# Where the sums for four conditioning vectors stand in the first mixer, and how many weight tiles they have

## The chip, the cores and the metric

One core of a Trainium2 chip. The metric is the device time of one execution in microseconds, the median of repeated runs. The core has TensorE (PE, with its weight loads PEld), VectorE (DVE), ScalarE (ACT), GpSimd (POOL) and SyncE (SP); POOL and SP issue most of the DMA transfers.

## What is computed

A two-layer trunk over 512 latent tokens and 256 context tokens, model width 1024, in float32. Layer 0 mixes tokens with a Fourier mixer beside a short gated convolution; layer 1 with windowed attention. Each layer ends in a mixture of 32 experts. Six vectors per layer and per stream shift, scale and gate the sub-layers, computed from the conditioning vectors:

```python
mod_l = (jax.nn.silu(c) @ w_mod[layer] + b_mod[layer])[:, None, :]
mod_c = jax.nn.silu(c_ctx) @ w_mod[layer] + b_mod[layer]
sh1_l, sc1_l, g1_l, sh2_l, sc2_l, g2_l = jnp.split(mod_l, 6, axis=-1)
```

The change concerns four of those of layer 1, `g1_l` to `g2_l` (numbers 2 to 5), each a product of one 1024 vector with a 1024 x 1024 block of `w_mod`. In layer 1 only the latent stream needs them.

## The kernel before

The kernel is one stream of Python calls on the five engines; a framework sets the order of each engine's instructions (the code's order is their priority, and a later one whose data is ready may go first) and puts in the waits. Tiles come from pools with a number of buffers per name; one more tile of a name waits until an older one is released. `tc.issue_after(ins)` orders the instructions issued in its block behind `ins`, those on the engine of `ins` alone.

**Modulation by TensorE** (`ModFeed`, L999). Twelve 2 MB tiles w of `w_mod` are loaded through POOL's queue (L1015) into two slots in turn, after four through SP's. Each `feed.step` multiplies one tile (L1037, 16 matmuls) and issues the load of the tile after next. These steps are called the modulation steps below.

**Modulation by VectorE** (`SumFeed`, L1047). The four vectors of layer 1 go as 32 steps, eight for each vector. A step takes one 512 KB tile mw of weights (loaded through POOL's queue, L1068; pool `sp`, two buffers), multiplies it by a number per partition and adds it to acc (L1077 for the first of eight, L1075 for the others), and issues the next load. After the eighth, `finish` (L1082) loads the bias row into another mw tile, sums acc over partitions with four matmuls (L1088, the column sum), adds the bias (two ops at L1090) and writes the vector to memory (L1091). acc is a single buffer.

**First mixer.** Eight chunks follow each other, each with projections of the normed tokens (`proj`, L1247: weights split into a high half by ScalarE at L1253 and a low half by VectorE at L1255, three buffers each; 48 matmuls at L1259 and L1260). The four Fourier chunks (g = 0 to 3, L1309) have one projection each and the Fourier matmuls and sums of the chunk before (`four_b`, L1269: L1276 on TensorE, U copied by ScalarE at L1277, Z by VectorE at L1281 to L1295, L1299 and L1302 on TensorE). The four convolution chunks (j = 0 to 3, L1330) have three projections each, and VectorE's ops for the gated convolution (L1350 to L1360). Two or three `feed.step` and, before the change, one to three `sums.step` stand in each chunk. Pool `fp` holds the Fourier tables, U and Z; it is closed in the first convolution chunk, and `cp` takes its memory.

**Behind the mixer**, `mixer_out` (L1368) splits the output weights (L1402, L1403), multiplies (L1436), reads gates and router vectors that the modulation wrote (gr L1395, md L1383; br L1374 is a bias row of the router), and the experts of layer 0 follow. Their weights are loaded by SP.

Of the kernel before, what the change touches and what calls it, by code (L numbers as in the profile page):

```python
# [10 lines left out]
F32 = mybir.dt.float32  # L11
# [9 lines left out]
D = 1024  # L21
# [64 lines left out]
def body(tc, I, out, upto=None, dbg=None):  # L86
# [3 lines left out]
    def pool(name, bufs=1, side="left", space=None):  # L90
        kw = dict(name=name, bufs=bufs, reuse_waits="tile")
        if space is None:
            kw["side"] = side
        else:
            kw["space"] = space
        g = tc.tile_pool(**kw)
        p = g.__enter__()
        p_close[id(p)] = g
        return p
# [146 lines left out]
    class Route:  # L246
# [7 lines left out]
        def __init__(self, NT, tb, t, psum, acc, spill, quads=0):  # L254
            self.NT, self.tb, self.t, self.psum, self.spill, self.quads = NT, tb, t, psum, spill, quads
            self.pairs = 16 - 2 * quads
            self.blocks = self.pairs + quads
            self.early = FIXED if quads else 16
            self.lower = []
            self.cuts = CUTS[NT]  # L260
            self.lg = t([128, NT, 36])
            self.gm = t([128, NT])
            self.og = t([128, NT, 4])
            self.mx = t([128, 2, NT, 4])
            self.M = t([128, 2, NT, 32])
            self.Mb = t([128, NT, 32], BF)
            self.Mc = t([128, 32], BF)
            self.rk = t([128, 2, NT])
            self.R = t([128, 2, NT, 32])
            self.oh = t([128, 2, NT, 64], BF)  # L270
            self.Mv = t([128, 2, 2, NT, 32], BF)
            n = max(b - a for a, b in zip((0,) + self.cuts, self.cuts + (NT,)))
            self.kg, self.gk, self.km = t([128, n, 4]), t([128, n]), t([128, n, 4])
            self.d, self.k, self.s2 = [t([128, n, 4, 8]) for _ in range(3)]
            self.acc = acc([128, 2, self.early])
# [723 lines left out]
    class ModFeed:  # L999
# [20 lines left out]
        def step(self, again=-1):  # L1020

            if self.cp >= len(self.todo):
                return
            l, g, q = self.todo[self.cp]
            w, i = self.wt.pop(self.cp)
            self.cp += 1
            if q == 0:
                bsrc = I["b_mod"][l, g * 2048:(g + 1) * 2048].rearrange("(q n) -> q n", q=4)
                for s in range(2):
                    G.dma_start(bm[s:128:32, :], bsrc)  # L1030
            first, last = (q == 0, q == 3) if self.whole else (True, True)
            if first:
                self.ps = self.psum_tile()
            for kk in range(2):
                k = 2 * q + kk
                for cb in range(4):
                    T.matmul(self.ps[cb * 32:cb * 32 + 32, :], sil[:, k, :], w[:, kk, cb * 512:cb * 512 + 512],  # L1037
                             start=first and kk == 0, stop=last and kk == 1)
            if again is not None:
                self.load(i if again < 0 else again)  # L1040
            if last:
                self.sum = V.tensor_add(bm, self.ps, bm)
            if q == 3:
                for s in range(2):
                    G.dma_start(mod_d[l, s, g * 2048:(g + 1) * 2048].rearrange("(q n) -> q n", q=4), bm[s:128:32, :])

    class SumFeed:  # L1047
# [1 line left out]


        def __init__(self, layer, vectors, room):
            self.layer, self.vectors, self.room = layer, vectors, room
            self.acc = room.tile([128, D], F32, name="acc")
            self.todo = [(v, k) for v in vectors for k in range(8)]
            self.w = []
            self.ld = 0
            for _ in range(2):
                self.load()

        def tile(self):  # L1060
            return self.room.tile([128, D], F32, name="mw", bufs=2)

        def load(self):
            if self.ld < len(self.todo):
# [5 lines left out]
        def step(self):  # L1070
            v, k = self.todo.pop(0)
            self.ld -= 1
            w = self.w.pop(0)
            if k:
                V.scalar_tensor_tensor(self.acc, w, sil[:, k, 0:1], self.acc, op0=ALU.mult, op1=ALU.add)  # L1075
            else:
                V.tensor_scalar(self.acc, w, sil[:, k, 0:1], None, op0=ALU.mult)  # L1077
            if k == 7:
                self.finish(v)
            self.load()  # L1080

        def finish(self, v):  # L1082

            ps, b = psB([128, 512]), self.tile()
            rows = b[0:64:32, 0:512]
            G.dma_start(rows, I["b_mod"][self.layer, v * D:(v + 1) * D].rearrange("(q n) -> q n", q=2))
            for r in (0, 32):
                T.matmul(ps[r:r + 32, :], onef.to_broadcast([128, 32]), self.acc[:, r * 16:r * 16 + 512], start=True, stop=True)  # L1088
            for r in (0, 32):
                V.tensor_add(b[r:r + 1, 0:512], ps[r:r + 1, :], b[r:r + 1, 0:512])  # L1090
            G.dma_start(mod_d[self.layer, 0, v * D:(v + 1) * D].rearrange("(q n) -> q n", q=2), rows)  # L1091
# [88 lines left out]
    mm = {}  # L1180
# [29 lines left out]
    sp = pool("sp", side="right")  # L1210
# [20 lines left out]
    def proj_pre():  # L1231
        ps = [psA([128, L + LC]) for _ in range(2)]
        for s in range(2):
            for g in range(2):
                if s == 0 and g == 1:
                    with tc.issue_after(mm["hi", 0, 4].ins):
                        split_pre(1)
                out = ps[g][:, s * L:L + s * LC]
                for i, (w, h) in enumerate(((0, hhi), (1, hhi), (0, hlo))):
                    for k in range(8):  # L1240
                        mm["last"] = T.matmul(out, wpre[:, g, w, k, :], h[s][:, k, :], start=k == 0 and i == 0, stop=k == 7 and i == 2)
            if s == 0:
                with tc.issue_after(mm["last"].ins):
                    feed.step()
        return ps
# [17 lines left out]
    def four_a(g):  # L1263
        ps = pre[g] if g < 2 else proj(lambda k0: wraw[:, k0:k0 + 4, g * 128:(g + 1) * 128])
        aT = tp.tile([128, L + LC + 4], F32, name="t3", bufs=2)
        S.copy(aT[:, 0:L + LC], ps)
        return aT
# [37 lines left out]
    prev = None  # L1305
    load_conv(0)
    pre = proj_pre()
    sums = SumFeed(1, (2, 3, 4, 5), sp)
    for g in range(4):  # L1309
        aT = four_a(g)  # L1310
        if g:
            with tc.issue_after(mm["last"].ins):
                feed.step()
        sums.step()
        if prev is not None:
            four_b(g - 1, prev)
        feed.step()
        sums.step()
        sums.step()
        prev = aT  # L1320
    wo = I["w_out_even"][0].rearrange("(j p) d -> p j d", p=128)

# [7 lines left out]
    for j in range(4):  # L1330
        wr4 = wconv[j]
        pc = proj(lambda k0: wr4[:, k0:k0 + 4, 1, :])
        if prev is not None:
            four_b(3, prev)
            prev = None
            close(fp)
            cp = pool("cp")
            u = cp.tile([128, L + LC + 4], F32, name="ut")
            for c in (0, L + 1, L + 2, L + LC + 3):
                V.memset(u[:, c:c + 1], 0.0)  # L1340
        csb = tp.tile([128, L + LC + 4], F32, name="t3", bufs=2)
        S.copy(csb[:, 0:L + LC], pc)
        feed.step()
        sums.step()
        load_conv(j + 1)
        if j == 3:
            wout = load_wout(0, 1)
        phv = proj(lambda k0: wr4[:, k0:k0 + 4, 2, :])
        for o, p0, n in segs:
            V.tensor_mul(u[:, o:o + n], csb[:, p0:p0 + n], phv[:, p0:p0 + n])  # L1350
        z = cp.tile([128, L + LC + 4], F32, name="z", bufs=2)
        S.activation(z[:, 1:1 + N2], u[:, 1:1 + N2], AF.Copy, scale=cw[:, 1, j:j + 1])
        V.scalar_tensor_tensor(z[:, 1:1 + N2], u[:, 0:N2], cw[:, 0, j:j + 1], z[:, 1:1 + N2], op0=ALU.mult, op1=ALU.add)
        V.scalar_tensor_tensor(z[:, 1:1 + N2], u[:, 2:2 + N2], cw[:, 2, j:j + 1], z[:, 1:1 + N2], op0=ALU.mult, op1=ALU.add)
        feed.step()
        sums.step()
        sums.step()
        pb = proj(lambda k0: wr4[:, k0:k0 + 4, 0, :])
        for o, p0, n in segs:
            V.tensor_mul(z[:, o:o + n], z[:, o:o + n], pb[:, p0:p0 + n])  # L1360
        put_y(4 + j, [z[:, o:o + 256] for o in (1, 257, L + 3)])
        feed.step()
        sums.step()
        sums.step()
    close(cp, tp, sp, hp)


# [646 lines left out]
```

## Time and profile before

| | |
|---|---|
| median of 3 runs | 1658.29 us (1654.82 to 1658.82) |
| profiled execution, its own time | 1657.86 us |
| its span | 1655.9 us |
| TensorE busy | 1525.1 us (92%) |
| VectorE busy | 759.7 us (46%) |
| ScalarE / POOL busy | 440.3 us / 141.7 us |
| DMA, mean over the span | 304 GB/s |

The span is that of one execution taken by the hardware profiler. An engine is busy while one of its instructions runs; instructions that issue DMAs are not counted as busy in this table. The time from a DMA's issue to its landing is given apart. Matmuls are pipelined and their ends are modelled. In a timeline the bracket at the end of a row gives the idle time before it and what ended it.

### The profile page before, as it was taken

How to read it: one execution, taken by the hardware profiler on the slowest of the kernel's cores; microseconds unless marked ns; L12 is line 12 of the kernel's file. 1: busy time of each engine (PE TensorE's matmuls, PEld its weight loads, DVE VectorE, ACT ScalarE, POOL GpSimd, SP SyncE). 2: the span in 40 equal slices, each digit the busy share in tenths (PEclk: the TensorE clock that was granted, in tenths of full speed). 3: DMA queues.
4: the chain of work that ended last, by engine and by line, in shares of the span. 5: the costliest groups of instructions: out<-in, count | busy, mean ns of one | idle time of the engine just before them, and what ended most of it. 6: DMA issues, size and time to landing. Idle time of an engine off the chain costs nothing.

```text
span 1655.9 us, 21500 instructions
## 1 busy us (share of the span) xinstructions
PE 1525.1 (92%) x8011; PEld 866.5 (52%) x8011; DVE 759.7 (46%) x1671; ACT 440.3 (27%) x879; POOL 141.7 (9%) x160
## 2 busy tenths in 40 slices
PE   4989997969999999999988989999799999997787
PEld 2757876843444434444447776668444544531332
DVE  4546553784342534333366975555622322320223
ACT  5322221311111111111046577644221222210110
POOL 2522100300000000000033210000000000000000
PEclk9999997979999999999979999999899999998999
DMA  9897672579999999999930121042699999999996
GB/s 387 306 389 246 229 245 82 189 278 424 425 424 424 381 394 424 425 424 424 407 121 1 51 52 52 1 128 76 237 426 427 426 426 427 426 416 427 426 427 260
DMA packets 108832, 503.50 MB, mean 304 GB/s; under 512 B 18784, under 2 KB 33632, under 8 KB 56752
## 3 DMA queue, kind: packets, MB, share of 16 engines
q1 hardware_dynamic: 93600, 447.31, 67.1%
q0 software_dynamic: 11952, 51.55, 8.2%
q10 hardware_dynamic: 3168, 3.17, 0.6%
q8 instruction: 66, 1.08, 0.3%
q14 instruction: 46, 0.38, 0.1%
HBM read 499.30 MB, written 5.32 MB: 305 GB/s over the span
## 4 chain that ended last, share of the span: by engine, by line
PE 34%; DMA 10%; DVE 3%; ACT 2%; issue 1%; SPq 0%; DVEq 0%; ACTq 0%
PE p L862 8%; PE yp L933 5%; DMA w<-in_w_dram 5%; DMA hhi<-in_w_dram 4%; PE A L1715 3%; PE cp L811 3%; PE A L1436 3%; PE tp L767 2%; PE A L1833 2%; PE O L1895 2%; PE B L1880 2%; ACT P L1839 1%; PE tp L774 1%; DVE x L812 1%; DMA w<-in_w_qkv_dram 0%
## 5 line engine op out<-in xcount | busy, mean ns | idle before, releaser
L862 PE MATMUL p<-w,xt 128*64 128x512 f32 (+1 forms) x1024 | 338.5, 611 | 14.3 <-DMA w<-in_w_dram 14.1
L862 PE MATMUL p<-r,xt 128*64 128x512 f32 (+1 forms) x784 | 284.2, 620 | 8.3 <-DMA r<-in_w_dram 7.9
L812 DVE TENSOR_TENSOR x<-x,cp 128x512 f32<-128x512 f32 x224 | 148.1, 685 | 96.5 <-PE cp L811 96.4
L875 DVE TENSOR_TENSOR sg<-sg,p 128x512 f32<-128x512 f32 x29 | 20.0, 688 | 365.9 <-PE p L862 354.9
L811 PE MATMUL cp<-y,ot 128*128 128x512 f32 x616 | 174.5, 419 | 8.3 <-DVE x L812 4.5
L862 PEld LDWEIGHTS p<-w,xt 128*64 128x64 f32 (+1 forms) x1024 | 99.6, 135 | 127.3 <-issue 98.6
L933 PE MATMUL yp<-w,ht 128*64 128x512 f32 (+1 forms) x512 | 158.7, 595 | 2.2 <-DMA w<-in_w_dram 2.2
L862 PEld LDWEIGHTS p<-r,xt 128*64 128x64 f32 (+1 forms) x784 | 84.5, 137 | 144.5 <-issue 124.8
L811 PEld LDWEIGHTS cp<-y,ot 128*128 128x128 f32 x616 | 107.2, 191 | 52.0 <-DVE x L812 26.3
L933 PE MATMUL yp<-r,ht 128*64 128x512 f32 (+1 forms) x368 | 128.7, 595 | 1.3 <-ACT ht L894 0.7
L799 ACT CAST y<-yp 128x512 fp32r<-128x512 f32 x58 | 34.0, 586 | 277.0 <-DVE yp L795 185.5
L1436 PE MATMUL A<-r,r 128*128 128x512 f32 x288 | 71.2, 404 | 2.2 <-ACT r L1402 1.4
L933 PEld LDWEIGHTS yp<-r,ht 128*64 128x64 f32 (+1 forms) x368 | 38.1, 134 | 66.7 <-issue 64.0
L862 PE MATMUL p<-hhi,xt 128*64 128x512 f32 (+1 forms) x128 | 66.0, 672 | 7.1 <-DMA hhi<-in_w_dram 7.1
L933 PEld LDWEIGHTS yp<-w,ht 128*64 128x64 f32 (+1 forms) x512 | 46.4, 131 | 45.6 <-issue 40.1
L1436 PEld LDWEIGHTS A<-r,r 128*128 128x128 f32 x288 | 55.1, 195 | 14.8 <-ACT r L1402 2.3
L1837 DVE CUSTOM_DVE_ANT_0 A<-A,band,nsink 128x640 f32<-128x640 f32 (+1 forms) x56 | 45.4, 831 | 35.4 <-PE A L1833 35.2
L865 ACT ACTIVATE sg<-p 128x512 f32<-128x512 f32 x29 | 17.3, 597 | 157.0 <-PE p L862 157.0
L801 DVE TENSOR_TENSOR y<-yp,y 128x512 fp32r<-128x512 f32 x58 | 40.1, 691 | 40.0 <-ACT y L799 40.0
L797 DVE SCALAR_TENSOR_TENSOR yp<-yp,gs,grow 128x512 f32<-128x512 f32 x26 | 19.7, 759 | 72.4 <-PE yp L933 72.4
L739 POOL DMA_INDIRECT r<-h_d,gi x17 | 17.0, 997 | 411.8 <-PE tp L774 342.4
L862 PE MATMUL p<-hlo,xt 128*64 128x512 f32 (+1 forms) x112 | 51.8, 611 | 0.0
(434 smaller groups left out, 2605.5 us busy)
## 6 DMA issues: line engine op xcount, KB each, us to landing
w<-in_w_dram SPq DMA_DIRECT2D x191, 1024.0 KB, 19.5
r<-in_w_dram SPq DMA_DIRECT2D x143, 1024.0 KB, 19.5
w<-in_w_mod_dram POOLq DMA_DIRECT2D x12, 2048.0 KB, 10.1
hhi<-in_w_dram SPq DMA_DIRECT2D x23, 1024.0 KB, 19.5
hlo<-in_w_dram SPq DMA_DIRECT2D x23, 1024.0 KB, 19.5
mw<-in_w_mod_dram POOLq DMA_DIRECT2D x32, 512.0 KB, 5.2
w<-in_w_in_even_dram SPq DMA_DIRECT2D x13, 512.0 KB, 11.2
w<-in_w_mod_dram SPq DMA_DIRECT2D x3, 2048.0 KB, 12.8
```

The source lines that it names most:

```text
L767: T.matmul(p, oh[:, m, :], near["h2"][m][i][:, hf * 512:hf * 512 + 512], start=n == 0, stop=n == 7)
L799: hi = S.copy(Yr[j, hf][0], ys)
L801: V.tensor_sub(Yr[j, hf][1], ys, Yr[j, hf][0].bitcast(F32))
L811: T.matmul(p, OT[j][:, m * 128:(m + 1) * 128], Yr[j, hf][i], start=n == 0 and i == 0, stop=n == len(js) - 1 and i == 1)
L812: return V.tensor_add(xs, xs, p)
L862: T.matmul(ps[rs], X[b][:, q, rs], W[j, wn, ab][:, q, :], start=q == 0, stop=q == 7)
L933: T.matmul(py_[hf][rs, :], HT[b][:, q % 4, rs], W[j, "w2", ab][:, q % 4, hf * 512:hf * 512 + 512], start=q % 4 == 0, stop=q % 4 == 3)
L1436: T.matmul(ps, lhs(m, a, j), whl[b][:, j, :], start=j == 0 and i == 0, stop=j == 7 and i == 2)
L1715: T.matmul(ps, h[st][:, k, ms], whl[k][b], start=k == 0 and i == 0, stop=k == 7 and i == 2)
L1833: T.matmul(ps[:, o0:o0 + w], qS[G_][:, c, b * 128:(b + 1) * 128], kS[part][:, 2 * G_ + c // 4, k0:k0 + w], start=part == 0, stop=part == 1)
L1837: V.tensor_tensor_reduce(out=ps[:, 0:w], in0=ps[:, 0:w], in1=bnd, op0=ALU.add, op1=ALU.min, scale=1.0, scalar=nsink[:, hd:hd + 1], accum_o ...
L1880: T.transpose(p[:, i, :], Ps[gl * 4 + i][:, t * 128:(t + 1) * 128], ident)
```

## The change

The object that holds the sums is made in the first Fourier chunk instead of ahead of the four, in an `issue_after` block that names the last matmul so far. It takes a list of pools and draws tiles from them in turn: from `sp` alone at first, from `sp` and `cp` (two buffers of mw in each) once `cp` is there, when two more loads are issued. The steps per chunk were 3, 3, 3, 3, 5, 5, 5, 5; they become 0, 1, 2, 3, 9, 9, 8, 0, the nine as three times three.

```diff
--- before.py
+++ after.py
@@ -1049,16 +1049,22 @@
 
 
         def __init__(self, layer, vectors, room):
-            self.layer, self.vectors, self.room = layer, vectors, room
+            self.layer, self.rooms, self.at = layer, [room], 0
             self.acc = room.tile([128, D], F32, name="acc")
             self.todo = [(v, k) for v in vectors for k in range(8)]
             self.w = []
             self.ld = 0
+            self.more()
+
+        def more(self, *rooms):
+
+            self.rooms += rooms
             for _ in range(2):
                 self.load()
 
         def tile(self):
-            return self.room.tile([128, D], F32, name="mw", bufs=2)
+            self.at += 1
+            return self.rooms[self.at % len(self.rooms)].tile([128, D], F32, name="mw", bufs=2)
 
         def load(self):
             if self.ld < len(self.todo):
@@ -1078,6 +1084,10 @@
             if k == 7:
                 self.finish(v)
             self.load()
+
+        def steps(self, n):
+            for _ in range(min(n, len(self.todo))):
+                self.step()
 
         def finish(self, v):
 
@@ -1305,18 +1315,18 @@
     prev = None
     load_conv(0)
     pre = proj_pre()
-    sums = SumFeed(1, (2, 3, 4, 5), sp)
     for g in range(4):
         aT = four_a(g)
         if g:
             with tc.issue_after(mm["last"].ins):
                 feed.step()
-        sums.step()
+        if g == 0:
+            with tc.issue_after(mm["last"].ins):
+                sums = SumFeed(1, (2, 3, 4, 5), sp)
         if prev is not None:
             four_b(g - 1, prev)
         feed.step()
-        sums.step()
-        sums.step()
+        sums.steps(g)
         prev = aT
     wo = I["w_out_even"][0].rearrange("(j p) d -> p j d", p=128)
 
@@ -1335,13 +1345,14 @@
             prev = None
             close(fp)
             cp = pool("cp")
+            sums.more(cp)
             u = cp.tile([128, L + LC + 4], F32, name="ut")
             for c in (0, L + 1, L + 2, L + LC + 3):
                 V.memset(u[:, c:c + 1], 0.0)
         csb = tp.tile([128, L + LC + 4], F32, name="t3", bufs=2)
         S.copy(csb[:, 0:L + LC], pc)
         feed.step()
-        sums.step()
+        sums.steps(3)
         load_conv(j + 1)
         if j == 3:
             wout = load_wout(0, 1)
@@ -1353,15 +1364,13 @@
         V.scalar_tensor_tensor(z[:, 1:1 + N2], u[:, 0:N2], cw[:, 0, j:j + 1], z[:, 1:1 + N2], op0=ALU.mult, op1=ALU.add)
         V.scalar_tensor_tensor(z[:, 1:1 + N2], u[:, 2:2 + N2], cw[:, 2, j:j + 1], z[:, 1:1 + N2], op0=ALU.mult, op1=ALU.add)
         feed.step()
-        sums.step()
-        sums.step()
+        sums.steps(3)
         pb = proj(lambda k0: wr4[:, k0:k0 + 4, 0, :])
         for o, p0, n in segs:
             V.tensor_mul(z[:, o:o + n], z[:, o:o + n], pb[:, p0:p0 + n])
         put_y(4 + j, [z[:, o:o + 256] for o in (1, 257, L + 3)])
         feed.step()
-        sums.step()
-        sums.step()
+        sums.steps(3)
     close(cp, tp, sp, hp)
```

## Rows read from the trace of the kernel before

**Rows 1.** Windows: length, busy PE, PEld, DVE, ACT, POOL, granted clock, DMA share, GB/s:

```profile
101.00:118.00 17.00, 11.37 (x71) 6.04 (x68) 7.88 (x16) 1.76 (x3) 5.57 (x10) 1.00 1.00 404
118.00:234.00 116.00, 116.00 (x693) 95.35 (x694) 68.84 (x102) 26.46 (x47) 18.63 (x34) 1.00 0.68 234
234.00:258.00 24.00, 12.80 (x56) 9.52 (x52) 8.97 (x17) 5.18 (x11) 0.54 (x1) 0.89 0.84 268
```

**Rows 2.** Timeline of TensorE, 98 to 118 us: start, us, engine, line, op:

```profile
104.44 1.92 PE L1037 MATMUL M<-w,sil 128*32 128x512 f32 x16 [3.40 <-DMA w<-in_w_mod_dram]
...
107.14 1.05 PE L1088 MATMUL B<-acc,onef 128*32 128x512 f32 x4 [0.77 <-DVE acc L1075]
...
110.99 1.93 PE L1037 MATMUL M<-w,sil 128*32 128x512 f32 x16
...
117.17 1.16 PE L1299 MATMUL A<-dl,Z 128*128 128x128 f32 x8 [1.45 <-DVE Z L1287]
```

**Rows 3.** Timeline of VectorE, 105 to 118 us:

```profile
105.80 1.28 DVE L1075 SCALAR_TENSOR_TENSOR acc<-mw,sil,acc 128x1024 f32<-128x1024 f32 x1 [4.34 <-DMA mw<-in_w_mod_dram]
...
112.49 0.75 DVE L1077 TENSOR_SCALAR acc<-mw,sil 128x1024 f32<-128x1024 f32 x1 [1.03 <-DMA mw<-in_w_mod_dram]
...
113.16 1.37 DVE L1090 TENSOR_TENSOR mw<-B,mw 1x512 f32<-1x512 f32 x2
...
116.70 0.41 DVE L1287 TENSOR_TENSOR Z<-U 128x256 f32<-128x256 f32 x1
```

**Rows 4.** Timeline of POOL, 60 to 102 us: DMA issues:

```profile
60.37 1.11 POOL L1068 DMA_DIRECT2D mw<-in_w_mod_dram  x2
...
95.15 0.75 POOL L1015 DMA_DIRECT2D w<-in_w_mod_dram  x1 [6.62 <-PE M L1037]
...
95.90 0.56 POOL L1068 DMA_DIRECT2D mw<-in_w_mod_dram  x1
...
101.37 0.75 POOL L1015 DMA_DIRECT2D w<-in_w_mod_dram  x1 [0.16 <-issue]
```

**Rows 5.** Tile w on POOL, in 95 to 96 and 101 to 102 us:

```profile
DMA to landing us min/median/max: 9.2/9.2/9.2
...
DMA to landing us min/median/max: 9.6/9.6/9.6
```

**Rows 6.** Tile acc: ns min/median/max, first and last start:

```profile
L1075 DVE SCALAR_TENSOR_TENSOR acc<-mw,sil,acc x28: 1274/1284/1286, 66.5 to 226.0; 128x1024 f32<-128x1024 f32 x28
...
L1077 DVE TENSOR_SCALAR acc<-mw,sil x4: 753/753/754, 64.6 to 202.2; 128x1024 f32<-128x1024 f32 x4
```

**Rows 7.** Timelines of VectorE, 150 to 190 us, and TensorE, 152 to 202 us:

```profile
156.65 0.75 DVE L1077 TENSOR_SCALAR acc<-mw,sil 128x1024 f32<-128x1024 f32 x1 [1.28 <-DMA mw<-in_w_mod_dram]
...
186.54 1.28 DVE L1075 SCALAR_TENSOR_TENSOR acc<-mw,sil,acc 128x1024 f32<-128x1024 f32 x1
...
154.37 1.03 PE L1088 MATMUL B<-acc,onef 128*32 128x512 f32 x4
...
199.19 1.05 PE L1088 MATMUL B<-acc,onef 128*32 128x512 f32 x4
```

**Rows 8.** Timeline of all engines, 232 to 262 us:

```profile
233.65 1.05 PE L1088 MATMUL B<-acc,onef 128*32 128x512 f32 x4
...
233.81 1.77 SPq L1490 DMA_DIRECT2D x<-in_x_dram  x4
...
236.07 1.19 PE L1436 MATMUL A<-r,r 128*128 128x512 f32 x4 [1.37 <-ACT r L1402]
...
244.07 8.57 SPq L1374 DMA_DIRECT2D br<-in_b_router_g_dram  x1
...
257.36 4.88 PE L1389 MATMUL B<-wr,md 128*128 128x36 f32 x22 [9.00 <-DMA md<-mod_d]
```

**Rows 9.** Waits, 56 to 245 us: who for whom, us in total, times, longest:

```profile
ACT whi L1253 <- PE A L1260: 70.0, 22, 5.6
...
DVE acc L1075 <- DMA mw<-in_w_mod_dram: 20.9, 13, 4.3
```

## The prediction, made before the changed kernel was run

> **What bounds the kernel now.** I read the windows by stage first, then TensorE's timeline around its one gap, then the queues that feed it. The windows [rows 1] show a first mixer that is TensorE's from 118 to 234 us: busy 116.00 of 116.00 us at granted clock 1.00, so nothing there can be shortened by moving VectorE's work; it can only be lengthened. Between 101 and 118 us TensorE is busy 11.37 of 17 us while the DMA share is 1.00. After 234 us it is idle for half the window. So the change can win in 101 to 118, and perhaps at the end.
>
> TensorE's timeline [rows 2] shows what the 101 to 118 gap is made of: 3.40 us before a modulation step at 104.44, released by a weight load w; 0.77 us before the column sum (L1088) of the first finished vector at 107.14, released by VectorE's acc; 1.45 us before the Fourier matmuls at 117.17, released by Z. Sum 5.62 us. The step at 110.99 shows no idle, but its w was issued at 101.37 and took 9.6 us [rows 4, 5]: it landed at 110.97, just in time. That matters below: whatever is gained ahead of it is lost again unless this w comes sooner.
>
> VectorE's rows [rows 3] show why Z is late: 112.49 acc starts the second vector after a wait of 1.03 us for its weights, 113.16 holds the two bias adds, and only then Z goes on, with the op that releases TensorE at 116.70.
>
> **The change, part by part.** The order of the code moves: before, 12 steps stand in the four Fourier chunks and 5 in each convolution chunk; now 0, 1, 2, 3, then 9, 9, 8, 0. The work is the same: 28 sums at 1284 ns, 4 first sums at 753 ns, four finishes [rows 6]. No byte and no instruction goes away; only the places differ. What holds a step to its place? Not the code's order alone: VectorE's 24th sum ran at 186.54 although its column sum ran on TensorE at 199.19, where the code has both [rows 7]. An instruction whose data is there runs ahead of its place. TensorE, always busy, keeps its places: the column sums stand where the code puts them, at 154.37 behind the third projection of the convolutions, at 199.19 behind the eighth [rows 7], at 233.65 behind the twelfth [rows 8]. That is (199.19 - 154.37) / 5 = 9.0 us a projection, modulation steps included. Since there is one acc, a column sum holds back all later steps. So the finishes are what really moves. By 9.0 us a projection: the first goes from 107.14 to behind the first projection (154.4 - 18, about 136), the second from 154.4 to behind the fourth (about 163), the third from 199.2 back to behind the sixth (about 181), the fourth from 233.65 to behind the ninth (about 208).
>
> *Finish one leaves the gap.* The 0.77 us wait and the 1.05 us of its matmuls go from 107.14, and acc and the bias adds (0.75 + 1.37 us) leave Z's way, so the 1.45 us [rows 2, 3] goes. If w lands at 110.97 as before, the first two gains are only waited away in front of that step, and 1.45 us is won. If the loads come sooner, all 5.62 us can go. The 1.05 us of matmuls comes back in the full stage: +1.05.
>
> *Loads taken out of 65 to 118 us.* The POOL queue lands in the order of issue: w of 95.15 took 9.2 us, to 104.4 [rows 4, 5], and the mw load issued behind it at 95.90 fed the sum that started at 105.80 [rows 3]. From there to 110.97, 5.2 us, the next 2 MB w had the queue, so an mw of 0.5 MB (the sizes are those of the tiles) takes a quarter, some 1.3 us. Eight mw loads were issued from 60.37 to 95.90, ahead of that w [rows 4]; the code's new order has five by then (two at the start, one and two after). So none to three fewer, 0 to 3.9 us; by the running ahead just shown, which is the nearest row, I take one: the w for 110.99 lands near 109.7, and the step gains 1.3 us.
>
> By the Trainium skill (DMA: Bandwidth & Descriptors, "Issuing engines are not separate DMA queues") transfers of all queues interleave on the same 16 engines; read strictly, the mw of 95.90 would delay the w ahead of it too, and the step at 104.44 would gain up to all 3.40 us with three loads gone. The landing order in this trace, 104.4 before 105.8, speaks for a line within POOL's queue, so the sum keeps 1.3.
>
> *The last chunk.* The fourth column sum, 1.05 us at 233.65, costs nothing now: TensorE then waits 1.37 us for ScalarE's r [rows 8]. Moved into the full stage it costs +1.05. VectorE gets 1.37 us (bias adds) back before its part of the weight split, so the output matmuls may start up to that much sooner. But TensorE then waits 9.00 us at 257.36 for md [rows 8], whose load stands on SP's queue behind br, which blocked 8.57 us at 244.07. Its row of loads begins at 233.81, when the last projection ends, and the DMA share over 234 to 258 is 0.84 [rows 1, 8]. That chain has no sum in it: output matmuls that start sooner only wait longer at 257. Gain 0; not below, since nothing is added there.
>
> *Four tiles and the bursts of three.* Two tiles more come from memory that the Fourier tables leave, so their first load waits for the last Fourier matmuls; the next one waits for a sum, since its pool's two are taken. Behind both on POOL's queue stand the last two w loads, and behind those the last two modulation steps on TensorE. A wait of a burst (3.9 us) there costs from nothing, if these loads were as early as their 9 to 10 us to land allow [rows 5], to 3.9; I take 0, since two steps' loads are always under way. A burst of three holds VectorE 3 x 1.28 = 3.85 us. Behind it on VectorE stand the low halves of the weights, for which ScalarE's casts waited 70.0 us in 22 places on TensorE [rows 9]: with three buffers they run two half projections, some 9 us, ahead. Cost 0 while a burst and its wait for mw stay under that. VectorE's waits for mw, 20.9 us in 13 places [rows 9], lose nothing on TensorE in 118 to 234 now, so shortening them wins nothing.
>
> **Sum.** -1.45 (Z) -1.3 (one load) +1.05 +1.05 (two column sums in the full stage) = -0.65 us. Bounds: loads as before, -1.45 + 2.10 = +0.65; whole gap gone, -5.62 + 2.10 = -3.5 (of it 3.40 by the three loads); whole gap gone and the column sums hidden, -5.6. The profiled execution took 1657.86 us (span 1655.92 and 1.94 around it), 0.43 below the median of the three runs shown, 1658.29. Forecast 1657.2. What is won by 234 us passes on to the end, as the later stages start when this one ends.
>
> **Rivals.** *A, the loads do follow the code.* Three mw loads fewer ahead of the two steps, and the second Fourier block of matmuls fills what wait is left: -3.5 us, 1654.4; at the bound of -5.6, 1652.3. For it: DMA is the full resource there, share 1.00 [rows 1]. Against: sums ran when data came, not by place.
>
> *B, slower: TensorE waits at the third column sum.* Sums 17 to 24 must now fit between the second and the third finish, about 163 to 181, 18 us. Before, with two tiles, they took from 156.65 to 187.8 (186.54 and 1.28), 31.2 us [rows 7]. With three free tiles (the fourth holds the bias row) 31.2 x 2/3 = 20.8: TensorE, in order, waits 2.8 us and the total is 1660.0; if depth does not help because the DMA is full, 31.2 - 18 = 13.2 us, 1670.4. It makes the kernel slower by over 0.3% once the eight sums take more than about 23.7 us. Against: the order on TensorE may put that column sum later, and then no one waits.
>
> *C, no move.* The block that is to delay the start names a TensorE instruction, while what it issues are POOL's loads, so that part does nothing; if the order comes out nearly as before, 1657.9.
>
> **How the numbers follow.** Chances: forecast 0.34, A 0.32, B 0.24, C 0.10. About 0.3%, 5.0 us, is what a measurement of this kernel can tell from no change. Faster than that: two thirds of A (0.21), since its bound and any shortening of the 9.00 us wait at 257 reach it, and 0.03 of the forecast: 0.24. Slower: three quarters of B (0.18) and 0.01 of the forecast: 0.19. Within: 0.57. The range goes from A's bound, 1652, to 1664, within B (between its 1660 and 1670); about 0.1 lies below and 0.1 above.
>
> **What would show it.** Right: no L1088 and no bias add before 118 us; the Fourier matmuls of 117.17 start 1.5 to 4 us sooner without a wait for Z; column sums near 136, 163, 181 and 208; none at 234; the wait for md still 9 to 10 us; TensorE still full in the convolutions. Wrong: idle time in front of L1088 or of a projection between 160 and 210 (B), a step at 104.44 without a wait (A), or a wait for md that is gone.

## The result and the profile after

The changed kernel takes 1638.49 us (median of 4 runs, 1635.07 to 1639.84) against 1658.55 us of the kernel before beside it: ratio 0.9884, 95% interval 0.9862 to 0.9906. The forecast was 1657.2, the range ended at 1652.0. The gain was forecast in the right direction and far too small, 0.65 us instead of some 20.

The spans of the two profiled executions are 1655.9 and 1637.7 us, 18.2 apart. The starts of TensorE's first and last instructions of some lines cut the execution into stretches in which both do the same work (first projection: first L1260; last projection: last L1260; md: first L1389; router: first matmul of L193, the transposes for the router's logits; attention of layer 1: first L1715 to the last L1895). Each length is the difference of two times read to 0.1 us. The last column is a second profile of the kernel before (the last run below); by it the 1.0 us of the first stretch are chance, and a difference of up to 1.9 us in the attention could be.

| stretch, us | before | after | difference | before again |
|---|---|---|---|---|
| start to the first projection | 72.0 | 73.0 | +1.0 | 73.2 |
| first to last projection | 161.4 | 156.5 | -4.9 | 161.4 |
| last projection to md's matmul | 24.0 | 16.9 | -7.1 | 23.5 |
| md to the router | 39.4 | 37.4 | -2.0 | 38.7 |
| router to the attention of layer 1 | 566.4 | 566.1 | -0.3 | 566.6 |
| attention of layer 1 | 236.8 | 232.0 | -4.8 | 234.9 |
| the rest | 555.9 | 555.8 | -0.1 | 555.3 |

So there are three places, and the forecast had a small part of the first. In the changed kernel the line numbers of the mixer are 10 higher, those behind it 9.

**First to last projection.** Windows of the kernel after, against [rows 1]; columns as there (busy PE, PEld, DVE, ACT, POOL, then the granted clock, DMA share, GB/s):

```profile
101.00:118.00 17.00, 17.00 (x112) 12.43 (x111) 11.38 (x27) 5.28 (x11) 3.50 (x6) 1.00 0.72 273
118.00:229.00 111.00, 111.00 (x661) 88.11 (x660) 67.19 (x92) 23.16 (x40) 21.94 (x39) 1.00 0.74 270
```

TensorE is full in both windows after the change. The step that [rows 2] leaves out before the gap:

```profile
99.11 1.92 PE L1037 MATMUL M<-w,sil 128*32 128x512 f32 x16
```

TensorE's timeline after, against [rows 2]:

```profile
100.10 4.48 PE L1286 MATMUL B<-dch,t 128*128 128x256 f32 x20
104.51 1.92 PE L1037 MATMUL M<-w,sil 128*32 128x512 f32 x16
106.36 1.13 PE L1286 MATMUL B<-dch,t 128*128 128x256 f32 x4
107.33 1.05 PE L1309 MATMUL A<-dl,Z 128*128 128x128 f32 x8
...
113.81 1.92 PE L1037 MATMUL M<-w,sil 128*32 128x512 f32 x16
...
125.21 1.05 PE L1098 MATMUL B<-acc,onef 128*32 128x512 f32 x4
```

Before, two modulation steps stood in a row, at 99.11 and 104.44, and the second waited 3.40 us for its w. Now 20 Fourier matmuls stand ahead of the first of the two (104.51), and the second runs at 113.81, when its w, issued at 96.23, has long landed (9.7 us after its issue, at 105.9). The loads did not come sooner. POOL's queue after, against [rows 4]:

```profile
61.41 1.11 POOL L1074 DMA_DIRECT2D mw<-in_w_mod_dram  x2
...
87.91 0.55 POOL L1074 DMA_DIRECT2D mw<-in_w_mod_dram  x1
...
96.23 0.75 POOL L1015 DMA_DIRECT2D w<-in_w_mod_dram  x1 [6.62 <-PE M L1037]
96.97 0.56 POOL L1074 DMA_DIRECT2D mw<-in_w_mod_dram  x1
```

Each stands 1.0 to 1.1 us behind its counterpart, as the first projection does (73.0 against 72.0), and up to 97 us there are eight mw loads, as before.

**Last projection to md.** SP's queue before, between the two rows shown in [rows 8], and the issue of md:

```profile
236.64 0.38 SPq L1395 DMA_DIRECT2D a<-mod_d  x1
237.12 0.46 SPq L1395 DMA_DIRECT2D h<-mod_d  x1
237.63 1.24 SPq L1395 DMA_DIRECT2D b<-mod_d  x1
242.28 0.33 SPq L723 DMA_DIRECT2D w<-in_w_dram  x1
242.71 0.56 SPq L1372 DMA_DIRECT2D wr<-in_w_router_g_dram  x1
...
254.40 0.38 SPq L1383 DMA_DIRECT2D md<-mod_d  x1
```

and after:

```profile
231.66 0.95 SPq L1499 DMA_DIRECT2D x<-in_ctx_dram  x2
232.66 0.56 SPq L1381 DMA_DIRECT2D wr<-in_w_router_g_dram  x1
233.26 3.90 SPq L1382 DMA_DIRECT2D wr<-in_w_router_e_dram  x1
237.21 3.27 SPq L1383 DMA_DIRECT2D br<-in_b_router_g_dram  x1
...
242.13 0.38 SPq L1392 DMA_DIRECT2D md<-mod_d  x1
...
243.54 0.46 SPq L1404 DMA_DIRECT2D a<-mod_d  x1
...
247.29 10.18 SPq L723 DMA_DIRECT2D w<-in_w_dram  x2
```

In the code wr comes first and a, h, b far behind it. The kernel before has a, h, b (512 KB each) and a weight tile w (1 MB) ahead of wr, br and md; the kernel after has them in the code's order. TensorE after, against [rows 8]:

```profile
232.12 11.17 PE L1445 MATMUL A<-r,r 128*128 128x512 f32 x48 [2.35 <-ACT r L1411]
246.45 2.05 PE L1398 MATMUL B<-wr,md 128*128 128x36 f32 x16 [3.15 <-DMA md<-mod_d]
249.14 13.03 PE L1445 MATMUL A<-r,r 128*128 128x512 f32 x44 [0.64 <-DVE x L1450]
```

The wait for md is 3.15 us where it was 9.00.

From md to the router TensorE runs in part at half clock (granted clock 0.5: 1.2 instead of 2.4 GHz); the last section gives what that costs.

**Theory S**, from these rows: the place that the framework gives a load on SP's queue depends on when its tile's memory is free. Pools that are opened later take the memory of closed ones. Pool `rq` (wr, br, gf, gr, md) lay over the memory of `sp` (acc, mw), which the fourth finish held to the end of the last chunk; pool `hq` (a, h, b) lay over `hp`, the normed tokens that the projections read, free at the last projection. (The expectation for the pools swapped calls them the projections' weights.) With the fourth finish one chunk sooner `sp` is free, and the code's order holds. It is the order set by the framework that counts, and not a wait in the run: before, the column sum had read acc by 234.70, and a still went out first, at 236.64. **Rival W**: the end is shorter because VectorE and the transfers have no sums left in the last chunk.

### The profile page after: what moved, and what is told of

It is laid out like the page before. It is cut to its first block, busy times and chain, and to the rows that moved or that the text cites. A ratio compares the mean times of both kernels' runs of the same rounds, so it can differ in the third digit from the quotient of the medians.

```text
span 1637.7 us, 21502 instructions
## 1 busy us (share of the span) xinstructions
PE 1522.8 (93%) x8011; PEld 863.4 (53%) x8011; DVE 753.9 (46%) x1671; ACT 439.9 (27%) x879; POOL 141.8 (9%) x160
## 4 chain that ended last, share of the span: by engine, by line
PE 33%; DMA 10%; DVE 3%; ACT 3%; issue 1%; SPq 0%; ACTq 0%; DVEq 0%
PE p L862 9%; PE yp L933 5%; DMA w<-in_w_dram 5%; DMA hhi<-in_w_dram 5%; PE cp L811 3%; PE A L1445 3%; PE A L1724 3%; PE tp L767 3%; PE O L1904 2%; PE A L1842 2%; PE B L1889 2%; ACT P L1848 1%; PE tp L774 1%; DVE x L812 1%; DMA w<-in_w_qkv_dram 0%
## 5 line engine op out<-in xcount | busy, mean ns | idle before, releaser
L865 ACT ACTIVATE sg<-p 128x512 f32<-128x512 f32 x29 | 17.3, 597 | 155.3 <-PE p L862 155.3
L862 PE MATMUL p<-hlo,xt 128*64 128x512 f32 (+1 forms) x112 | 55.2, 644 | 0.0
## 6 DMA issues: line engine op xcount, KB each, us to landing
hhi<-in_w_dram SPq DMA_DIRECT2D x23, 1024.0 KB, 18.7
```

The lines of the kernel that those rows point to most:

```text
L862: T.matmul(ps[rs], X[b][:, q, rs], W[j, wn, ab][:, q, :], start=q == 0, stop=q == 7)
```

## The experiments

The results of one group stand against the kernel before on the same chip. There it took 1653.80, 1654.88 and 1654.91 us and not 1658.3, on which the expectations' totals in us are built; these are to be read some 4 us lower. The changed kernel itself, run with the second group, gives the scale: 1636.38 us, ratio 0.9878 [0.9857, 0.9899].

> The changed kernel itself, unedited, beside the others on one chip. Every theory: 0.986 to 0.991 of the kernel before; md's matmul 16.9 us behind the last projection.

### The pools swapped, no sum moved

```diff
-    hq = pool("hq", side="right")
     rq = pool("rq", side="right")
+    hq = pool("hq", side="right")
...
-    close(rq, hq, pp)
+    close(hq, rq, pp)
```

> The kernel before with one edit: the two memory pools of the output stage that are opened at the end of the first mixer are opened in the other order, so that the router's rows (wr, br, gf, gr, md) lie where the projections' weights lay, and the three broadcast rows a, h, b lie where the sums' acc and mw lay. No sum is moved. Theory S (what held md back was that its row's memory was under acc, held until the fourth finish, so that a, h, b and a weight load went first on SP's queue): the x loads are followed at once by wr; the last projection still ends at 233.7 us; md's matmul starts about 250 instead of 257.4 (16.7 us behind the last projection, as in the changed kernel, instead of 23.6), the half-clock stretch is shorter by about 2 us, and the attention stage of layer 1, whose order on the engines follows the changed kernel's here, gives back some 4.8 us more: total 1643 to 1647 us. Rival W (the end of the mixer is shorter because VectorE and the transfers have no sums left there): no gain at the end, 1653 to 1659 us (the lower end if the attention order alone gives its 4.8 us).

1647.02 us against 1653.80, ratio 0.9953 [0.9936, 0.9969]. SP's queue and md's matmul:

```profile
239.52 0.56 SPq L1372 DMA_DIRECT2D wr<-in_w_router_g_dram  x1
...
249.04 0.38 SPq L1383 DMA_DIRECT2D md<-mod_d  x1
...
251.49 0.87 SPq L1395 DMA_DIRECT2D a<-mod_d  x1
```

```profile
253.62 3.63 PE L1389 MATMUL B<-wr,md 128*128 128x36 f32 x16 [3.97 <-DMA md<-mod_d]
```

With the twelve and twenty sums where they were, the order on the queue up to md is that of the changed kernel, and md comes 17.3 us behind the last projection (before 24.0 and 23.5, after 16.9 and 17.2). W is out for this stretch. The attention of layer 1 took 231.6 us, as in the changed kernel, so the total is not md's gain alone. It fell by 6.8 us, less than the 11 to 15 that S expected below 1658. Two pieces are missing. The last projection began at 236.3 and not at 233.4, the first at 73.3 and not at 72.0: in this execution TensorE went at half clock in part of the gap that is left in the Fourier chunks (granted clock 0.80 in 101 to 118; 1.00 and 0.90 in the two profiles of before). And from md to the router it took 39.4 us, as before, though less of it ran at half clock: here 41 of the 180 output matmuls (L1436) up to the router stand ahead of md and 139 behind it, where the kernels before and after have 48 and 132. Seven matmuls at the 0.23 us that one takes ahead of md (48 in 11.17 us) are 1.6 us that only changed their stretch.

### The last chunk emptied, nothing else

The kernel before with `steps(n)` of the change, in the three places of a convolution chunk:

```diff
-        sums.step()
+        sums.steps(2 if j < 3 else 0)
...
-        sums.step()
-        sums.step()
+        sums.steps((3, 3, 2, 0)[j])
...
-        sums.step()
-        sums.step()
+        sums.steps(2 if j < 3 else 0)
```

> The kernel before with the last convolution chunk emptied of sums and nothing else: 12 steps in the four Fourier chunks as before, then 7, 7, 6, 0 in the convolution chunks, two weight tiles. Theory S: the Fourier gap of 101 to 118 us stays and the last projection ends where it did or one column sum later, 233.7 to 234.8 us; the loads on SP's queue stand as in the changed kernel, md's matmul starts about 251, and the total is 1644 to 1648 us. Rival W expects a gain at the end too, but without the queue's order as its cause (that is for the swap of pools to tell). Rival F (the gain was made in the Fourier chunks): 1656 to 1659 us.

1642.68 us, ratio 0.9930 [0.9913, 0.9947]. First to last projection 162.7 us, that is 161.4 and the column sum that is now inside; md 16.8 us behind; attention of layer 1 231.4. The gap of 101 to 118 us stays (TensorE busy 11.62 of 17). More than half of the change's gain needs no sum moved out of the Fourier chunks and no third and fourth tile.

### The changed kernel with its last sum kept late

The first edit stands in the first and in the second place of a convolution chunk, the second in the third.

```diff
-        sums.steps(3)
+        sums.steps(3 if j < 3 else 0)
...
-        sums.steps(3)
+        sums.steps(3 if j < 2 else 1)
```

> The changed kernel with one step kept back: the last of the 32 sums, and with it the fourth finish, stands at the end of the last convolution chunk (9, 9, 7, 1). Four tiles, Fourier chunks as changed. Theory S: a, h, b and a weight load go ahead of wr on SP's queue again; the last projection ends within 1 us of the changed kernel's 229.8; md's matmul starts about 253 to 255 instead of 246.5, and the total is 8 to 10 us above the changed kernel: 1646 to 1649 us. Rival W: one sum and one finish at the end cost what they last, 1.3 + 1.05 + 1.4 us: at most 1642 us. In both the attention stage of layer 1 lasts as in the changed kernel.

1644.22 us, ratio 0.9936 [0.9920, 0.9953]; the changed kernel has 0.9878, so one sum and its finish cost 0.0058, some 9.6 us (each ratio against its own group's kernel before). The last projection ended at 228.3, 1.5 us sooner than in the changed kernel, where 1 us was expected: the fourth column sum stands behind it. Queue and TensorE:

```profile
231.35 0.38 SPq L1404 DMA_DIRECT2D a<-mod_d  x1
...
236.68 0.33 SPq L723 DMA_DIRECT2D w<-in_w_dram  x1
237.10 0.56 SPq L1381 DMA_DIRECT2D wr<-in_w_router_g_dram  x1
```

```profile
251.70 7.01 PE L1398 MATMUL B<-wr,md 128*128 128x36 f32 x32 [8.92 <-DMA md<-mod_d]
```

md is 23.7 us behind the last projection, as in the kernel before. W's limit of 1642 is passed.

### The changed kernel with a, h, b issued ahead of wr

```diff
+        if layer == 0:
+            ahb = [row(hq, "a2", ...), row(hq, "h2", ..., bufs=3), row(hq, "b2", ...)]
         wr = rq.tile([128, 8, 36], F32, name="wr")
```

> The changed kernel with the loads of the rows a, h and b (512 KB each, broadcast to 128 partitions) issued ahead of wr, br, gf, gr and md on SP's queue; no sum is moved. Theory S: md comes later by about what these three take on the queue, 5 to 7 us, and the total is 1643 to 1648 us. Rival W (the place of the sums makes the gain, not the queue): 1637 to 1640 us.

1644.98 us, ratio 0.9943 [0.9926, 0.9959]. Every sum is where the change has it, and md is 21.2 us behind the last projection instead of 16.9: 4.3 us for three loads of 512 KB, less than the 5 to 7 that were expected. With the w of 1 MB ahead too it was 6.8 (the run above). Between 240 and 250 us the DMA moved 381 GB/s in the profile of before, share 1.02: by that rate 1.57 MB take 4.1 us and 2.62 MB 6.9. So md pays for the bytes ahead of it, by this estimate. The kernel before has one more thing on the queue: it stood still from 238.87 to 242.28, ahead of w, whose memory VectorE's r (L1403) released. The transfers ahead ran on meanwhile, at 400 GB/s and share 1.02, so that stop cost md little.

### Seven sums in the Fourier chunks, two tiles

```diff
-        sums.step()
...
-        sums.step()
-        sums.step()
+        sums.steps((1, 2, 2, 2)[g])
```

The step behind four_a and the two behind four_b become none and 1, 2, 2, 2; the convolution chunks have 7, 7, 6, 5.

> The kernel before with seven sums in the Fourier chunks instead of twelve (none behind four_a; 1, 2, 2, 2 behind four_b), so that the first finish stands in the first convolution chunk, and 7, 7, 6, 5 after them; two weight tiles, sums up to the end of the last chunk. Theory S, part Fourier (the gap of 101 to 118 us goes because without a finish in these chunks the Fourier matmuls stand ahead of the second modulation step in TensorE's order, and not because loads come sooner): mw loads are issued at the same times as before (eight ahead of 98 us), yet TensorE is full in 101 to 118 and the last projection ends 4 to 5 us sooner than before, counted from the first projection's start. Rival L (fewer mw loads ahead of the w loads are needed): the gap stays, as the loads do. At the end, by S, a, h, b stand ahead of wr, and md's matmul comes 23 to 24 us behind the last projection, as before. Attention stage of layer 1 as in the changed kernel, 4.8 us less than before. Total 0.993 to 0.996 of the kernel before by S; by L 0.996 to 0.999.

1647.01 us, ratio 0.9946 [0.9926, 0.9967]. POOL issued eight mw loads up to 97 us here too, the last at 96.87, and the gap is gone:

```profile
101.00:118.00 17.00, 17.00 (x112) 12.43 (x111) 11.30 (x27) 5.18 (x11) 2.62 (x4) 1.00 0.71 266
```

```profile
99.99 4.48 PE L1280 MATMUL B<-dch,t 128*128 128x256 f32 x20
104.40 1.92 PE L1037 MATMUL M<-w,sil 128*32 128x512 f32 x16
...
228.93 1.05 PE L1092 MATMUL B<-acc,onef 128*32 128x512 f32 x4 [0.45 <-DVE acc L1075]
```

Rival L is out: the loads are the same, the order is that of the changed kernel, and it came with the first finish and five sums out of these chunks. The edit does not part these two, and why the framework then puts the Fourier matmuls first is not shown. From the first to the last projection it takes 155.3 us, 6.1 less than before and more than the 4 to 5 that were expected, since the fourth column sum stays outside. Where that finish is late, md is 23.6 us behind, as before.

### The changed kernel with two tiles

```diff
             cp = pool("cp")
-            sums.more(cp)
```

> The changed kernel with two weight tiles instead of four; all sums stand in the code where the change puts them. Theory S: the order of SP's queue decides; here the fourth finish comes out at the end of the last projection again, and a, h, b go ahead of wr: md's matmul 23 to 24 us behind the last projection, total 8 to 10 us above the changed kernel, as with the last sum kept late (0.992 to 0.995 of the kernel before). Rival T (two more tiles change nothing, since TensorE is full either way): within 3 us of the changed kernel.

1646.17 us, ratio 0.9939 [0.9918, 0.9959]: 9.8 us above the changed kernel of the same group, though the code asks for the sums in the same places. With two tiles the fourth column sum is put behind the last projection again, a, h, b and w go ahead, and md is 23.6 us behind. The two tiles more shorten nothing on TensorE by themselves; they let the fourth finish come early.

### The attention of layer 1 in another order, the mixer as before

```diff
-        for f, d in ((st_norm, 0), (st_kv, 1), (st_kt, 3)):
+        for f, d in ((st_norm, 0), (st_kt, 3), (st_kv, 1)):
```

> The kernel before with one line of the attention stage of layer 1 edited: in its pipeline the key parts are written ahead of the key and value projections instead of behind them. Nothing of the first mixer, of SP's queue or of the experts of layer 0 is moved; what the scheduler then puts out for the second part of the stage (the query parts) is the order of the changed kernel, and for the first part one that neither kernel has. Theory O (the attention stage's 4.8 us come from the order of its instructions alone, a by-product of the scheduling, and the sums have no part in it): md's wait, the half clock and everything up to 860 us as before; the second part, from the last projection of L1715 to the last of L1895, takes 130 us instead of 132.5, the first part 101 to 105: total 2 to 5 us less than before, ratio 0.997 to 0.999. Rival C (the stage is shorter because it starts sooner, or because memory or transfers of the first mixer reach into it): as before, ratio 0.999 to 1.001.

1653.04 us (11 runs) against 1654.91, ratio 0.9990 [0.9981, 0.9999]. The stage's second part takes 129.6 us, as theory O expected: the last L1715 starts at 966.0 and the last L1895 at 1095.6, where the kernel before and after have

```profile
L1715 PE MATMUL A<-w,hhi x128: 388/396/795, 863.2 to 967.5; 128*128 128x512 f32 x128
...
L1895 PE MATMUL O<-w,v x144: 592/593/644, 985.6 to 1100.0; 128*64 128x512 f32 x144
```

```profile
L1724 PE MATMUL A<-w,hhi x128: 388/396/792, 849.9 to 951.9; 128*128 128x512 f32 x128
...
L1904 PE MATMUL O<-w,v x144: 592/592/644, 967.2 to 1081.9; 128*64 128x512 f32 x144
```

(minimum, median and maximum in ns, first and last start): 132.5 before, 130.0 after. The order alone makes these 2.5 us; rival C is out for this part. In it TensorE's order by line is the same in all profiles; ScalarE's and VectorE's are those of the changed kernel here. The total agrees, if only just: 1.9 us less, and its interval ends at 0.9999. For the first part (104.3 before, 102.0 after, 103.2 here) the two profiles of before differ by 1.6 us, 104.3 and 102.7, so up to some 2 us there stay open.

### The small rows first on the queue

The changed kernel, with gf and, for layer 0, md and gr loaded ahead of wr and br:

```diff
+        gf = rq.tile([128, 8], F32, name="gf")
+        Y.dma_start(gf, ...)
+        pre = {}
+        if layer == 0:
+            for s in range(2):
+                t = rq.tile([128, 2, 8], F32, name=f"md{s}")
+                Y.dma_start(t, ...)
+                pre[s] = t, row(rq, "gr", ..., bufs=2)
         wr = rq.tile([128, 8, 36], F32, name="wr")
```

> The changed kernel with the loads of gf, md and gr (the small rows) put ahead of wr and br on SP's queue at the end of the first mixer; nothing else is moved. Theory S (md's place on the queue sets when TensorE goes on): wr's second load blocked the queue 3.90 us and br's first 3.27 us, so md lands some 7 us sooner and is no longer what TensorE waits for; it then waits for wr, landing near 241 instead of 246.5, 3 to 5 us gained, half of them perhaps lost to the next wait (x, a, gfr): 1 to 5 us under the changed kernel. Rival W: no change, within 1 us.

1632.62 us (1632.13 to 1634.41) where the changed kernel beside it took 1636.38 (1635.00 to 1637.74): 3.8 us less, the ranges apart, ratio to before 0.9856 [0.9836, 0.9875]. This beats both kernels.

```profile
233.73 0.61 SPq L1390 DMA_DIRECT2D md<-mod_d  x1
...
240.96 1.00 SPq L1395 DMA_DIRECT2D wr<-in_w_router_e_dram  x1
```

```profile
244.71 2.17 PE L1410 MATMUL B<-wr,md 128*128 128x36 f32 x18 [0.98 <-DMA wr<-in_w_router_g_dram]
```

As expected, TensorE now waits for wr and not for md, but wr landed later than the 241 of the expectation: the matmul came 14.8 us behind the last projection, 2.1 sooner than in the first profile of the changed kernel. A further 2.6 us was won behind it (2.1 against the profile of the changed kernel in the same group), where no half clock is left (below).

### The kernel before again

> The kernel before itself, unedited, to see how far its profile repeats. Every theory: md's matmul 23 to 25 us behind the last projection, half clock for 10 us or more behind it, and 236 to 238 us from the first to the last attention projection of layer 1.

1655.64 us, one run. md 23.5 us behind the last projection, half clock from about 252 to 269. The attention stage took 234.9 us, a little below the 236 that was expected; the ten profiles with another order lie between 230.7 and 232.8.

## Why the prediction was wrong

- *"Gain 0" for the last chunk* is the step that failed: "That chain has no sum in it". The chain of loads on SP's queue has no sum in it, but the memory that its tiles wait for was held by the sums. Measured in its place: -7.1 us up to md, and -2.0 from md to the router, where 2.8 us less were lost to the half clock. The rows were there to read. The forecast took the x loads at 233.81 and the blocked br at 244.07 from the queue and left out the rows between, in which a, h, b and w stand ahead of wr against the code's order. A load that is not where the code has it asks for the reason, and that reason was acc and mw, held by the fourth finish.
- *Finish one leaves the gap*: right that the wait for Z goes and that no L1088 or bias add is left before 118. The forecast's bound "whole gap gone", -5.62, is what happened, and not through loads: of the one load that the forecast took (-1.3) and the three of rival A nothing came, since the loads are driven by the sums' data, as the forecast itself had argued. The steps' order on TensorE changed: the Fourier matmuls went ahead of a whole modulation step, and the Fourier matmuls on Z of 117.17 came at 107.33, where 1.5 to 4 us sooner was forecast. Rival A had Fourier matmuls fill a wait, but behind fewer loads; its sign, a step near 104.44 without a wait, came without its cause. The first column sum's +1.05 was counted wrongly for this case: its matmuls left a place in the same stretch, and with no idle time around only the fourth, which came in from behind the last projection, adds 1.05. -5.62 + 1.05 = -4.57, measured -4.9; with the fourth kept late, -6.1 and -6.2 (155.3 and 155.2 us) against -5.62. The 0.3 to 0.6 us that are left over stay open.
- The rule of the Trainium skill weighed there (DMA: Bandwidth & Descriptors, "Issuing engines are not separate DMA queues") could not decide anything: with the same loads in flight no run here shows what fewer of them would have given.
- *Positions*: column sums forecast at 136, 163, 181, 208, measured at 125.21, 165.35, 190.24 and 214.65. The last three came later than forecast, yet early enough for the end. Rival C was right on one point: the block that was to delay the start delays no load, as the first mw loads show (61.41 and 60.37, no more apart than the first projections).
- *Rival B* did not come: VectorE waited for mw 2.8 us in 2 places instead of the 20.9 in 13 of [rows 9], TensorE for no column sum. The eight sums of the third vector took from 167.86 to 186.57, 18.7 us instead of 31.2.
- *What is won by 234 us passes on* held up to the attention: from the router to there the two kernels differ by 0.3 us. The attention of layer 1 was in no case of the forecast, so its -4.8 us came by luck. No line of it was changed, but it came out in another order, worth 2.5 us in one part and up to 2 more in the other.

## What to carry to other kernels

Before a stall at a load is called independent of a change, compare the queue's order with the code's; where they differ, ask which tile's memory each load waits for and who held it last. Moving work out of the last stretch of a stage can be worth far more than its own time, when it frees memory that the next stage's first loads need. And a change to the places of a few instructions may reorder stages that it does not touch: cut two traces into stretches of equal work, count the instructions in each, and look where the difference is made before giving it a cause.

## What was not expected of the hardware

The half clock (1.2 instead of 2.4 GHz) is a second price of such a wait. Windows from md's matmul to the router, of the kernel before, of the kernel after, of the one with the small rows first and of the one with the pools swapped (behind the counts the granted clock, then the DMA share):

```profile
257.36:296.83 39.47, 39.47 (x165) 33.59 (x166) 17.65 (x30) 6.00 (x10) 0.00 (x0) 0.84 0.18 57
```

```profile
246.45:283.78 37.33, 36.69 (x164) 30.58 (x165) 18.03 (x30) 6.04 (x10) 0.00 (x0) 0.91 0.38 130
```

```profile
244.71:279.51 34.80, 34.19 (x164) 28.42 (x165) 17.70 (x28) 6.06 (x10) 0.00 (x0) 1.00 0.42 137
```

```profile
253.62:292.98 39.36, 39.36 (x172) 33.16 (x173) 18.14 (x30) 6.05 (x10) 0.00 (x0) 0.89 0.32 124
```

From the last projection to md TensorE had been idle for 11.2 us (1.37, 0.83 and 9.00), 5.5 us (2.35 and 3.15), 3.3 us (2.35 and 0.98) and 6.2 us (1.37, 0.82 and 3.97). The half clock that came with it lasted 17.1, 6.8, 0 and 10.2 us in all; in the third the clock did not fall. A stretch at clock c loses (1 - c) of its length against full clock: some 6.2 (its clock is 0.844), 3.4, 0 and 4.3 us here. Without that and without TensorE's idle time in it (0.64 us in the second, 0.61 in the third) the stretches are 33.3, 33.3, 34.2 and 35.1 us long, the last with seven matmuls more, some 1.6 us. The same sum gives 33.3 to 33.5 us in the other eight profiles, one of them (the last chunk emptied) with two matmuls more. So the half clock explains what the stretch from md to the router gains or loses, but for some 0.9 us with the small rows first, which stay open.

By the Trainium skill (TensorE: Matmul & The Clock Gate, "HAM oscillation — how this bites in real kernels") matmuls behind a long enough wait for a transfer run at the low clock, and what that costs is half of the time at that clock. The trace agrees: between the kernels before and after the time lost that way differs by 2.8 us, the idle time by 0.64 the other way, and the stretch by 2.1.
